# One row of weights ahead in the mixing, kept low parts and regrouped loads, in a two-layer hybrid decoder kernel

## The chip, the core and the metric

The kernel runs on one core of one Trainium2 chip. The metric is device time in microseconds (us) from the start to the end of one execution; several runs are timed, and one execution more is taken with the hardware profiler. TensorE (PE) multiplies matrices and loads its weights beside that (PEld), VectorE (DVE), ScalarE (ACT) and GpSimd (POOL) do the elementwise work, and SyncE (SP) issues the transfers (DMAs).

## The reference

Two layers of a decoder trunk on 1024 tokens of width 1024, in float32. Each layer has a token mixing and a channel mixing, each between a norm before and a norm after, whose scale, shift and gate come from a condition vector `c` (adaLN):

```python
mod = silu(c) @ ada_w[l] + ada_b[l]                # 6 x 1024: shift, scale, gate, for each half
h = rms_norm(x, g_pre_mix[l]) * (1 + scale_m) + shift_m
q, k, v, u = split(h @ w_in[l] + b_in[l])          # widths 512, 128, 128, 512
attn = sliding_window_attention(rotary(q), rotary(k), v, sinks)   # window 128, 8 heads on 2
pool = causal_pool_mixer(u)                        # trailing means over 2/4/8/16 less the token
x = x + gate_m * rms_norm(concat(attn, pool) @ w_out[l], g_post_mix[l])
h = rms_norm(x, g_pre_ffn[l]) * (1 + scale_f) + shift_f
f = (silu(h @ w_gate[l]) * (h @ w_up[l])) @ w_down[l]             # inner width 2816
x = x + gate_f * rms_norm(f, g_post_ffn[l])
```

## The kernel before

Every product of float32 matrices is made of three matmuls on parts: `split` rounds a tile to its high part `hi` on ScalarE (L213) and subtracts it from the tile on VectorE, which leaves the low part `lo` (L214); `mm3` adds high x high, high x low and low x high in one accumulator (L239, L242, L243). `weight` loads one row block of weights (128 rows) into a part of a `raw` tile and splits it. `raw`, `hi` and `lo` tiles are handed out in parts by `part`: there are two `raw` tiles of four 512-wide parts, and three `hi` and three `lo` tiles of two parts. Accumulators are four banks `acc` of PSUM, and smaller products share three banks `msc`.

The 1024 tokens are worked on in two halves of 512. In each layer the stages follow one another as generators, which `run` interleaves step by step:

- `dense0`: query and key/value projections of half 0 (`q_pass`, `kv_pass`).
- `dense`: `u_pass` of half 0 (the pooling mixer's input), then `kv_pass` and `q_pass` of half 1, 20 blocks of weight rows in all, with the attention of half 0 and the pooling mixer (`pool_mix`) between their steps. L797 to L822 are the softmax, L928 to L938 the pooling's sums.
- `out0`: the output projection of half 0 (`natural_proj`, called by `mix_out`), in two column halves `nh` of eight steps `k`. Each step splits a block of `w_out` and the block `left[k]` of the concatenated attention and pooling results, again for the second column half. The attention of half 1 is interleaved.
- `u_pass` of half 1, with the attention of half 1 and the norm of half 0 behind it; then first products of the channel mixing (`firsts`), and `out1`, the output projection of half 1.
- The rest of `firsts`, beside the norm of half 1 and `up_sums`, which builds for eight blocks the sums and differences of token halves (in pairs, on VectorE at L997 and L1002, on GpSimd at L1000 and L1004) that the products by seven instead of eight use, and splits them.
- `ups`: 11 pairs of columns of the up and gate weights, five products each (`up_pair`): raw weights of a pair are loaded (L1071), summed on VectorE (L1101, L1102, L1106, L1107), split and multiplied.
- `down`: the down projection by seven products. Its operand B11 is loaded into tiles `hT` by six loads (L1147), which are written in the last pair of `ups`.

The adaLN vectors of later stages are a stream of their own at the side (`side`): `ada_sum` loads blocks of `ada_w` into two `ar` tiles of 256 KB each and adds them up on VectorE, scaled by a column of `c_act` (L271, L273).

Each engine takes its instructions from a queue in a fixed order. That order is not the order of the text: the program builder schedules the instructions when the kernel is built, by data dependencies, free tiles and its own costs. `after(ins, prev)` forces one instruction to stand behind another.

In `q_pass`, `kv_pass` and `u_pass`, a row block is loaded and split in the step that multiplies by it, except for the first two passes of layer 0, which ask one step ahead (`ahead`).

## Time and profile before

| | us |
|---|---|
| Runs, median (each) | 1931.88 (1932.43, 1927.65, 1931.88) |
| The profiled execution's own time | 1928.41 |
| Span of the profile | 1926.6 |
| TensorE busy | 1867.8 (97%) |
| VectorE busy | 1559.5 (81%) |
| ScalarE busy | 949.8 (49%) |
| GpSimd busy | 49.1 (3%) |

Busy is the time in which an engine has an instruction at work; shares are of the span. Matmuls overlap in the pipeline, so a step between the starts of two matmuls is shorter than one matmul's duration. In the trace's rows the bracket behind an instruction tells how long its engine was idle before it and what it waited for.

### The profile page before, as it was taken

The numbers are of one execution on the slowest core, as the hardware profiler recorded it, in microseconds if no ns is written. First come the engines' busy times: TensorE is split into PE (matmuls) and PEld (weight loads), VectorE is DVE, ScalarE is ACT, GpSimd is POOL, SyncE is SP. The second block draws the span as 40 slices with busy tenths as digits, with TensorE's granted clock in tenths as the row PEclk, the third lists the DMA queues.
The fourth block names the chain that finished last, engine by engine and source line by source line (L and its number), as shares of the span: only waits on it lengthen the run. The fifth ranks groups of instructions, "written<-read, shape, count | busy, mean of one in ns | idle before, by whom it ended". The sixth has DMA issues, their size and how long they took to land.

```text
span 1926.6 us, 26083 instructions
## 1 busy us (share of the span) xinstructions
PE 1867.8 (97%) x8978; PEld 1540.6 (80%) x8978; DVE 1559.5 (81%) x2906; ACT 949.8 (49%) x1789; POOL 49.1 (3%) x100
## 2 busy tenths in 40 slices
PE   6999999999999999999999999999999999999997
PEld 4787778887788888888887878788878888888886
DVE  5889976758889898788878998756788888867687
ACT  4775785654222223445658667755622222235452
POOL 1000000011000000000000000000200000000000
PEclk9999999999999999999999999999999999999999
DMA  9345563558445565844554465536684555474342
GB/s 327 98 154 152 156 227 119 180 168 282 161 164 195 177 212 182 295 147 147 170 168 136 123 179 176 174 110 202 199 276 153 187 196 180 150 252 156 115 151 101
DMA packets 227428, 341.86 MB, mean 177 GB/s; under 512 B 16952, under 2 KB 124360, under 8 KB 227296
## 3 DMA queue, kind: packets, MB, share of 16 engines
q1 hardware_dynamic: 227152, 340.17, 53.8%
q8 instruction: 70, 1.15, 0.2%
q14 instruction: 62, 0.51, 0.1%
q0 software_dynamic: 32, 0.00, 0.0%
q10 hardware_dynamic: 112, 0.04, 0.0%
HBM read 267.25 MB, written 72.89 MB: 177 GB/s over the span
## 4 chain that ended last, share of the span: by engine, by line
PE 74%; DVE 12%; DMA 6%; ACT 4%; issue 2%; POOL 0%; SPq 0%; DVEq 0%; ACTq 0%; POOLq 0%
PE acc L243 23%; PE acc L239 22%; PE acc L242 22%; DMA ar<-in_ada_w_dram 3%; DVE lo L214 2%; DVE ada L273 1%; DMA raw<-in_w_up_dram 1%; PE msc L832 1%; ACT hi L213 1%; PE msc L502 1%; PE pv L239 1%; PE pv L242 1%; DMA ar<-x 1%; DVE fn L541 1%; PE pv L243 1%
## 5 line engine op out<-in xcount | busy, mean ns | idle before, releaser
L213 ACT ACTIVATE hi<-raw 128x1024 fp32r<-128x1024 f32 (+1 forms) x388 | 332.2, 868 | 374.5 <-PE acc L242 203.1
L214 DVE TENSOR_TENSOR lo<-raw,hi 128x1024 fp32r<-128x1024 f32 (+1 forms) x388 | 381.2, 989 | 122.6 <-ACT hi L213 122.1
L243 PE MATMUL acc<-t,lo 128*128 128x512 f32 x704 | 275.4, 391 | 5.0 <-DVE lo L214 5.0
L239 PE MATMUL acc<-t,hi 128*128 128x512 f32 x704 | 275.0, 391 | 1.6 <-ACT hi L213 1.6
L242 PE MATMUL acc<-t,hi 128*128 128x512 f32 x704 | 274.6, 390 | 0.0
L239 PE MATMUL acc<-bh,hi 128*128 128x512 f32 x520 | 202.7, 390 | 0.0
L243 PE MATMUL acc<-bh,lo 128*128 128x512 f32 x520 | 202.4, 389 | 0.0
L239 PE MATMUL acc<-hT,hi 128*128 128x512 f32 x480 | 190.6, 397 | 8.7 <-ACT hi L213 6.5
L242 PE MATMUL acc<-hT,hi 128*128 128x512 f32 x480 | 188.0, 392 | 0.0
L243 PE MATMUL acc<-hT,lo 128*128 128x512 f32 x480 | 186.2, 393 | 0.8 <-DVE lo L214 0.7
L1086 DVE TENSOR_TENSOR fn<-acc,fn 128x512 f32<-128x512 f32 x220 | 150.3, 683 | 42.6 <-PE acc L243 42.1
L243 PEld LDWEIGHTS acc<-t,lo 128*128 128x128 f32 x704 | 132.5, 188 | 35.0 <-DVE lo L214 7.6
L239 PEld LDWEIGHTS acc<-t,hi 128*128 128x128 f32 x704 | 132.6, 188 | 30.7 <-ACT hi L213 3.1
L242 PEld LDWEIGHTS acc<-t,hi 128*128 128x128 f32 x704 | 132.5, 188 | 27.7
L242 PE MATMUL acc<-ph,hi 128*128 128x512 f32 x320 | 124.6, 389 | 0.0
L273 DVE SCALAR_TENSOR_TENSOR ada<-ar,c_act,ada 128x512 f32<-128x512 f32 x140 | 104.4, 746 | 18.0 <-DMA ar<-in_ada_w_dram 16.7
L1024 ACT ACTIVATE fn<-fn 128x512 f32<-128x512 f32 x44 | 27.8, 633 | 177.3 <-DVE fn L1086 177.3
L243 PEld LDWEIGHTS acc<-bh,lo 128*128 128x128 f32 x520 | 97.6, 188 | 20.4
L239 PEld LDWEIGHTS acc<-bh,hi 128*128 128x128 f32 x520 | 97.6, 188 | 20.2
L239 PEld LDWEIGHTS acc<-hT,hi 128*128 128x128 f32 x480 | 90.3, 188 | 28.8 <-ACT hi L213 8.8
L243 PEld LDWEIGHTS acc<-hT,lo 128*128 128x128 f32 x480 | 89.8, 188 | 20.4 <-DVE lo L214 2.5
L242 PEld LDWEIGHTS acc<-hT,hi 128*128 128x128 f32 x480 | 90.3, 188 | 16.8
(306 smaller groups left out, 3870.9 us busy)
## 6 DMA issues: line engine op xcount, KB each, us to landing
ar<-in_ada_w_dram SPq DMA_DIRECT2D x160, 256.0 KB
raw<-in_w_gate_dram SPq DMA_DIRECT2D x44, 512.0 KB
raw<-in_w_up_dram SPq DMA_DIRECT2D x44, 512.0 KB
raw<-in_w_in_dram SPq DMA_DIRECT2D x80, 256.0 KB
raw<-keeps SPq DMA_DIRECT2D x40, 512.0 KB
keeps<-fn SPq DMA_DIRECT2D x66, 256.0 KB
two_b<-in_w_down_dram SPq DMA_DIRECT2D x30, 512.0 KB
raw<-keepa SPq DMA_DIRECT2D x25, 512.0 KB
```

The lines of the kernel that those rows point to most:

```text
L213: nc.scalar.activation(hi, src, AF.Copy)
L214: nc.vector.tensor_sub(lo, src, hi.bitcast(F32))
L239: ins = nc.tensor.matmul(dst, lh, rh, start=first, stop=False)
L242: nc.tensor.matmul(dst, lh, rl, start=False, stop=False)
L243: return nc.tensor.matmul(dst, ll, rh, start=False, stop=last)
L273: nc.vector.scalar_tensor_tensor(acc, w, c_act[:, i : i + 1], acc, op0=ALU.mult, op1=ALU.add)
L502: ins = nc.tensor.transpose(bank[:, t * P : (t + 1) * P], src[t], ident)
L541: nc.vector.scalar_tensor_tensor(fn[t][:, cs], fn[t][:, cs], rstd[:, t : t + 1], xs[t][:, cs], op0=ALU.mult, op1=ALU.add)
L832: nc.tensor.transpose(bank[:, i * P : (i + 1) * P], s[:, ii, ck * P : (ck + 1) * P], ident)
L1024: nc.scalar.activation(g, g, AF.Silu)
L1086: nc.vector.tensor_add(halves_of(dst)[m], bank, halves_of(src)[m])
```

## The change

Five edits:

1. `split` remembers its VectorE instruction, and every accumulation of `ada_sum` is forced behind the split that was written last.
2. `one_ahead` takes a list of row blocks across the borders of passes and hands out one at each step, after having loaded and split the next. All passes of the mixing take their rows from it.
3. `natural_proj` keeps the low parts of `left[k]`, `k` under 6, of the first column half in tiles `uT` and `pt`, and makes only their high parts again in the second.
4. The two GpSimd subtractions of `up_sums` go to VectorE.
5. The six loads of B11 are written one in each of the last six pairs of `ups`, each forced behind that pair's last raw load.

```diff
+    recent = {}
+
     def split(hi, lo, src):
 
         nc.scalar.activation(hi, src, AF.Copy)
-        nc.vector.tensor_sub(lo, src, hi.bitcast(F32))
+        recent["split"] = nc.vector.tensor_sub(lo, src, hi.bitcast(F32))
...
+    def one_ahead(makers):
+
+        makers = iter(makers)
+        held = [next(makers)()]
+
+        def ask():
+            now_ = held.pop()
+            for make in makers:
+                held.append(make())
+                break
+            return now_
+
+        return ask
...
-                    nc.vector.tensor_scalar(acc, w, c_act[:, 0:1], None, op0=ALU.mult)
+                    ins = nc.vector.tensor_scalar(acc, w, c_act[:, 0:1], None, op0=ALU.mult)
                 else:
-                    nc.vector.scalar_tensor_tensor(
+                    ins = nc.vector.scalar_tensor_tensor(
                         acc, w, c_act[:, i : i + 1], acc, op0=ALU.mult, op1=ALU.add
                     )
+                after(ins, recent["split"])
...
         K = len(left)
+        lows = {}
         for nh in range(2):
...
                 wh, wl = weight(*wsrc(k, nh))
-                lh, ll = part("hi"), part("lo")
-                split(lh, ll, left[k])
+                lh = part("hi")
+                if k in lows:
+                    ll = lows[k]
+                    nc.scalar.activation(lh, left[k], AF.Copy)
+                else:
+                    if nh == 0 and k < 6:
+                        lows[k] = t_("uT" if k < 4 else "pt", [P, HALO + T], F32R)[:, :T]
+                    ll = lows[k] if k in lows else part("lo")
+                    split(lh, ll, left[k])
...
-    def u_pass(l, h, hT, cols, uts, piece_read):
+    def u_pass(l, h, hT, cols, uts, piece_read, ask):
         banks = [acc_bank() for _ in range(4)]
         for k in range(KD):
-            wh, wl = weight((ALLP, None, w_in[l, k * P : (k + 1) * P, QKV:INW]))
+            wh, wl = ask()
...
-        nc.gpsimd.tensor_sub(f0, f1, f0)
+        nc.vector.tensor_sub(f0, f1, f0)
         split(*ops[T3][k], f0)
         nc.vector.tensor_sub(f1, f1, b11)
         split(*ops[T2][k], f1)
-        nc.gpsimd.tensor_sub(b21, b21, f1)
+        nc.vector.tensor_sub(b21, b21, f1)
...
+        ask = one_ahead(
+            (all_rows(q_rows, l) + all_rows(kv_rows, l, 2) if l else [])
+            + all_rows(u_rows, l) + all_rows(kv_rows, l, 2) + all_rows(q_rows, l)
+        )
...
-        run(u_pass(l, 1, pieces, cols, uts[1], lambda k, ins: None), KD, (att, 10), (pre, KD))
+        ask1 = one_ahead(all_rows(u_rows, l))
+        run(u_pass(l, 1, pieces, cols, uts[1], lambda k, ins: None, ask1), KD, (att, 10), (pre, KD))
...
-                    if p == NPAIR - 1 and i == 1:
-                        for g in range(len(DOWN_GROUPS)):
-                            load(B11, g)
+                    g = p - (NPAIR - len(DOWN_GROUPS))
+                    if g >= 0 and i == 1:
+                        after(load(B11, g), recent["raw"])
                     yield
```

Line numbers of the changed kernel are higher: L216 there is L214 of before, L287 and L289 are L271 and L273, L816 to L841 are L797 to L822, L947 to L957 are L928 to L938, L696 is L667, L1023 is L1004, L1044 is L1025, L1073 is L1054, L1122, L1123, L1127 and L1128 are L1101, L1102, L1106 and L1107.

The order of instructions on VectorE, first in `dense` of layer 0, where `u_pass` ends and the row blocks of `kv_pass` are wanted. Before:

```order
L932 SCALAR_TENSOR_TENSOR pt<-pt,uT 128x512
L797 ISA sb,st<-msc,mask 128x256
L797 ISA st 128x1
L737 TENSOR_TENSOR vz<-qkv,vz 128x64 x2
L797 ISA sb,st<-msc,mask 128x256
L797 ISA st 128x1
L817 TENSOR_TENSOR st<-st 128x4
L937 TENSOR_TENSOR pt<-pt,rcnt 128x16
L273 SCALAR_TENSOR_TENSOR ada<-ar,c_act,ada 128x512
L818 RECIPROCAL st<-st 128x4
L938 TENSOR_TENSOR pt<-pt,uT 128x16
L214 TENSOR_TENSOR lo<-raw,hi 128x512
```

In the changed kernel, the rows that lead up to the same softmax (`vz`, L756 there, is L737):

```order
L216 TENSOR_TENSOR lo<-raw,hi 128x512
L828 SCALAR_TENSOR_TENSOR st<-st,sk 128x4
L947 TENSOR_TENSOR pt<-pt 128x525
L831 TENSOR_TENSOR st<-st,sk 128x4
L947 TENSOR_TENSOR pt<-pt 128x521
L756 TENSOR_TENSOR vz<-qkv,vz 128x64 x2
L816 ISA sb,st<-msc,mask 128x256
L816 ISA st 128x1
L816 ISA sb,st<-msc,mask 128x256
L816 ISA st 128x1
L951 SCALAR_TENSOR_TENSOR pt<-pt,uT 128x512
L216 TENSOR_TENSOR lo<-raw,hi 128x512
```

The low part of a row stands ahead of the pooling's last sums and of the softmax's reciprocal, and no accumulation of adaLN stands between the two low parts.

Second, on VectorE at the end of the first `kv_pass` of layer 1, where the bias is added to keys and values (L667). Before:

```order
L484 TENSOR_SCALAR cfb<-sa,rs 128x1024
L484 TENSOR_SCALAR cfb<-sb,rs 128x1024
L273 SCALAR_TENSOR_TENSOR ada<-ar,c_act,ada 128x512 x2
L214 TENSOR_TENSOR lo<-raw,hi 128x512
L273 SCALAR_TENSOR_TENSOR ada<-ar,c_act,ada 128x512 x2
L667 TENSOR_TENSOR qkv<-acc,bqkv 128x256 x4
```

And in the changed kernel (L501 is L484):

```order
L501 TENSOR_SCALAR cfb<-sa,rs 128x1024
L501 TENSOR_SCALAR cfb<-sb,rs 128x1024
L289 SCALAR_TENSOR_TENSOR ada<-ar,c_act,ada 128x512
L696 TENSOR_TENSOR qkv<-acc,bqkv 128x256 x4
L739 TENSOR_TENSOR rt<-qkv,cos_t 128x80
```

Three accumulations and the split of a row no longer stand ahead of the bias additions; that split stands further up.

Third, on VectorE at the start of `ups`, where the first sums of the up weights are made. Before:

```order
L1025 TENSOR_TENSOR sb<-sb 128x512
L1101 TENSOR_TENSOR raw<-raw 128x8x128
L271 TENSOR_SCALAR ada<-ar,c_act 128x512
L1102 TENSOR_TENSOR raw<-raw 128x8x128
L273 SCALAR_TENSOR_TENSOR ada<-ar,c_act,ada 128x512
L1106 TENSOR_TENSOR raw<-raw 128x8x128
L214 TENSOR_TENSOR lo<-raw,hi 128x1024
L273 SCALAR_TENSOR_TENSOR ada<-ar,c_act,ada 128x512
```

And in the changed kernel:

```order
L1044 TENSOR_TENSOR sb<-sb 128x512
L1122 TENSOR_TENSOR raw<-raw 128x8x128
L1123 TENSOR_TENSOR raw<-raw 128x8x128
L1127 TENSOR_TENSOR raw<-raw 128x8x128
L216 TENSOR_TENSOR lo<-raw,hi 128x1024
L1073 TENSOR_TENSOR sb<-acc,sa 128x512
L1128 TENSOR_TENSOR raw<-raw 128x8x128
L1073 TENSOR_TENSOR sb<-acc,sa 128x512
```

The accumulations between the sums and the low part are gone from this place; the first of them stands some rows further down.

## Rows read from the trace of the kernel before

**Rows 1.** The engines' busy time over the span, with instruction counts (first part of the profile's page).

```profile
PE 1867.8 (97%) x8978; PEld 1540.6 (80%) x8978; DVE 1559.5 (81%) x2906; ACT 949.8 (49%) x1789; POOL 49.1 (3%) x100
```

**Rows 2.** Stretches of the span: from and to, length, busy us (instructions) of TensorE, its weight loads, VectorE, ScalarE and GpSimd, then the granted clock of TensorE (1.00 is full), the busy share of the DMA engines and what they moved in GB/s. The first two, the sixth and the seventh lie in the mixing of the two layers; the third is the time before the up products of layer 0, the fourth their start, the fifth their long part, and the last their start in layer 1.

```profile
62.00:170.00 108.00, 101.16 (x634) 86.45 (x634) 98.08 (x295) 78.80 (x195) 4.92 (x13) 0.98 0.42 125
...
201.00:236.00 35.00, 33.73 (x184) 26.98 (x183) 33.50 (x88) 26.06 (x68) 0.42 (x2) 1.00 0.53 166
...
415.00:455.00 40.00, 40.00 (x190) 33.34 (x190) 36.52 (x46) 25.54 (x41) 11.39 (x8) 1.00 0.69 210
455.00:500.00 45.00, 42.08 (x176) 33.37 (x175) 38.51 (x51) 13.83 (x16) 0.00 (x0) 0.96 0.73 250
500.00:950.00 450.00, 450.00 (x2001) 372.23 (x2000) 382.09 (x516) 165.05 (x237) 0.00 (x0) 1.00 0.56 189
1014.00:1048.00 34.00, 31.70 (x191) 26.20 (x191) 32.10 (x106) 28.77 (x70) 0.00 (x0) 1.00 0.35 99
...
1148.00:1181.00 33.00, 31.83 (x170) 26.26 (x171) 28.97 (x81) 24.22 (x63) 0.48 (x2) 1.00 0.44 137
...
1400.00:1445.00 45.00, 41.36 (x177) 33.02 (x178) 39.00 (x50) 13.62 (x16) 0.00 (x0) 1.00 0.81 279
```

**Rows 3.** TensorE's waits by line and what they waited for: us in total, times, the longest.

```profile
PE acc L239 <- ACT hi L213: 9.9, 10, 2.2
PE acc L243 <- DVE lo L214: 5.6, 7, 1.1
PE msc L832 <- DVE sb L822: 5.2, 7, 1.3
```

**Rows 4.** TensorE's timeline at the places that the prediction speaks of: start, duration, instruction, in brackets the idle time before it and its releaser.

```profile
83.99 0.50 PE L239 MATMUL acc<-hT,hi 128*128 128x512 f32 x1 [2.18 <-ACT hi L213]
...
84.57 0.39 PE L239 MATMUL acc<-hT,hi 128*128 128x512 f32 x1
84.79 0.40 PE L242 MATMUL acc<-hT,hi 128*128 128x512 f32 x1
...
150.39 0.50 PE L242 MATMUL acc<-lo,hT 128*128 128x512 f32 x1 [2.32 <-DVE lo L214]
...
151.31 0.67 PE L239 MATMUL msc<-hi,pwh 128*128 128x512 f32 x1
...
154.33 0.63 PE L242 MATMUL acc<-lo,hT 128*128 128x512 f32 x1
...
456.16 0.50 PE L239 MATMUL acc<-t,hi 128*128 128x512 f32 x1 [0.76 <-ACT hi L213]
...
458.95 0.63 PE L243 MATMUL acc<-t,lo 128*128 128x512 f32 x1
...
461.51 0.63 PE L243 MATMUL acc<-t,lo 128*128 128x512 f32 x1
...
1015.38 0.50 PE L239 MATMUL acc<-hT,hi 128*128 128x512 f32 x1 [1.47 <-DVE qkv L667]
...
1149.17 0.50 PE L239 MATMUL acc<-hi 128*128 128x512 f32 x1 [1.47 <-ACT hi L213]
```

**Rows 5.** VectorE's timeline in `dense` of layer 0, up to the low part that the matmul of 150.39 waits for, in the same columns.

```profile
143.09 0.75 DVE L273 SCALAR_TENSOR_TENSOR ada<-ar,c_act,ada 128x512 f32<-128x512 f32 x1 [1.35 <-DMA ar<-in_ada_w_dram]
...
146.42 0.74 DVE L273 SCALAR_TENSOR_TENSOR ada<-ar,c_act,ada 128x512 f32<-128x512 f32 x1
...
148.84 0.74 DVE L273 SCALAR_TENSOR_TENSOR ada<-ar,c_act,ada 128x512 f32<-128x512 f32 x1
...
149.65 0.68 DVE L214 TENSOR_TENSOR lo<-raw,hi 128x512 fp32r<-128x512 f32 x1
150.25 0.87 DVE L822 TENSOR_SCALAR sb<-sb,st 128x256 f32<-128x256 f32 x3
```

**Rows 6.** ScalarE's timeline ahead of the high part that the matmul of 83.99 waits for.

```profile
79.43 1.28 ACT L813 ACT_TABLE_LOAD   x1
...
83.33 0.61 ACT L213 ACTIVATE hi<-raw 128x512 fp32r<-128x512 f32 x1
```

**Rows 7.** VectorE's timeline in layer 1 ahead of the matmul of 1015.38.

```profile
1012.76 0.75 DVE L273 SCALAR_TENSOR_TENSOR ada<-ar,c_act,ada 128x512 f32<-128x512 f32 x1 [1.32 <-DMA ar<-in_ada_w_dram]
...
1014.58 1.41 DVE L667 TENSOR_TENSOR qkv<-acc,bqkv 128x256 f32<-128x256 f32 x4
```

**Rows 8.** VectorE's low parts of `left[k]` by their operands, over the whole span: count, durations in ns (least, median, greatest), first and last start.

```profile
L214 DVE TENSOR_TENSOR lo<-cfa,hi x32: 661/681/687, 167.3 to 1172.2; 128x512 fp32r<-128x512 f32 x32
L214 DVE TENSOR_TENSOR lo<-cfb,hi x32: 679/684/694, 316.2 to 1301.8; 128x512 fp32r<-128x512 f32 x32
```

**Rows 9.** The timeline of all engines in `up_sums` of layer 0, where GpSimd and VectorE work at the same time.

```profile
428.24 1.67 POOL L1004 TENSOR_TENSOR ar<-ar,sa 128x512 f32<-128x512 f32 x1 [0.80 <-DVE sa L1002]
428.68 2.38 DVE L214 TENSOR_TENSOR t<-sa,t 128x512 fp32r<-128x512 f32 x2
...
430.99 0.68 DVE L214 TENSOR_TENSOR t<-ar,t 128x512 fp32r<-128x512 f32 x1
```

**Rows 10.** VectorE's timeline at the start of `ups` in layer 0.

```profile
452.26 1.23 DVE L1101 TENSOR_TENSOR raw<-raw 128x1024 f32<-128x1024 f32 x1 [0.57 <-DMA raw<-in_w_up_dram]
...
454.94 0.75 DVE L273 SCALAR_TENSOR_TENSOR ada<-ar,c_act,ada 128x512 f32<-128x512 f32 x1
```

More of the change, by code (lines that the diff above doesn't have):

```diff
@@ L633, in hybrid_decoder_kernel, with kv_rows, q_rows, u_rows @@
     attn = {}
-    def kv_pass(l, hT, par, qkvs, pairs=None):
+    def kv_rows(l, k):
+        return weight(
+            (ALLP, 2, w_in[l, k * P : (k + 2) * P, ATT:QKV].rearrange("(a p) n -> p a n", p=P))
+        )
+    def q_rows(l, k):
+        return weight((ALLP, None, w_in[l, k * P : (k + 1) * P, 0:ATT]))
+    def u_rows(l, k):
+        return weight((ALLP, None, w_in[l, k * P : (k + 1) * P, QKV:INW]))
+    def all_rows(rows, l, step=1):
+        return [lambda k=k: rows(l, k) for k in range(0, KD, step)]
+    def kv_pass(l, hT, par, qkvs, ask, pairs=None):
         banks = pairs or [acc_bank() for _ in range(2)]
         dsts = [banks[t // 2][:, t % 2 * 256 : t % 2 * 256 + 256] for t in range(NT)]
-        def rows(k):
-            return weight(
-                (ALLP, 2, w_in[l, k * P : (k + 2) * P, ATT:QKV].rearrange("(a p) n -> p a n", p=P))
-            )
-        ahead = None
-        if pairs:
-            ahead = rows(0)
-            yield
         for k in range(KD):
             if k % 2 == 0:
-                (wh, wl), ahead = ahead or rows(k), None
-            elif pairs and k + 1 < KD:
-                ahead = rows(k + 1)
+                wh, wl = ask()
             cs = slice(k % 2 * 256, k % 2 * 256 + 256)
@@ L667, in kv_pass, with q_pass @@
             nc.vector.tensor_add(qkvs[t][:, ATT:QKV], dsts[t], par["bq"][:, ATT:QKV])
-    def q_pass(l, hT, par, qkvs, first=False):
+    def q_pass(l, hT, par, qkvs, ask):
         banks = [acc_bank() for _ in range(NT)]
-        def rows(k):
-            return weight((ALLP, None, w_in[l, k * P : (k + 1) * P, 0:ATT]))
-        ahead = None
-        if first:
-            ahead = rows(0)
-            yield
         for k in range(KD):
-            wh, wl = ahead or rows(k)
-            ahead = rows(k + 1) if first and k + 1 < KD else None
+            wh, wl = ask()
             hi, lo = hT[k]
@@ L688, in q_pass @@
             nc.vector.tensor_add(qkvs[t][:, 0:ATT], banks[t], par["bq"][:, 0:ATT])
-    def u_pass(l, h, hT, cols, uts, piece_read):
+    def u_pass(l, h, hT, cols, uts, piece_read, ask):
         banks = [acc_bank() for _ in range(4)]
         for k in range(KD):
-            wh, wl = weight((ALLP, None, w_in[l, k * P : (k + 1) * P, QKV:INW]))
+            wh, wl = ask()
             for g in range(4):
@@ L1070, in up_pair @@
             for m, w in enumerate((w_gate, w_up)):
-                nc.sync.dma_start(raws[kh][:, m * HK : (m + 1) * HK, :], up_rows(w, l, kh, 2 * p, 2 * p + 2))
+                recent["raw"] = nc.sync.dma_start(
+                    raws[kh][:, m * HK : (m + 1) * HK, :], up_rows(w, l, kh, 2 * p, 2 * p + 2)
+                )
         (a11, a21), (a12, a22) = ((r[:, :, 0:P], r[:, :, P : 2 * P]) for r in raws)
@@ L1146, in load @@
             w = t_(tag, [P, p1 - p0, 512])
-            nc.sync.dma_start(w, rows[odd][:, p0:p1, dh * 512 : (dh + 1) * 512])
             wd[name].append(w)
+            return nc.sync.dma_start(w, rows[odd][:, p0:p1, dh * 512 : (dh + 1) * 512])
         return wd, load
@@ L1363, in dense0 @@
         def dense0():
-            yield from q_pass(l, hts[0], par, qkvs[0]) if l else queries0
-            yield from kv_pass(l, hts[0], par, qkvs[0]) if l else keys0
+            yield from q_pass(l, hts[0], par, qkvs[0], ask) if l else queries0
+            yield from kv_pass(l, hts[0], par, qkvs[0], ask) if l else keys0
+        ask = one_ahead(
+            (all_rows(q_rows, l) + all_rows(kv_rows, l, 2) if l else [])
+            + all_rows(u_rows, l) + all_rows(kv_rows, l, 2) + all_rows(q_rows, l)
+        )
         side = ada_jobs(l)
@@ L1373, in dense @@
         def dense():
-            yield from u_pass(l, 0, hts[0], cols, uts[0], piece_read)
-            yield from kv_pass(l, pieces, par, qkvs[1])
-            yield from q_pass(l, pieces, par, qkvs[1])
+            yield from u_pass(l, 0, hts[0], cols, uts[0], piece_read, ask)
+            yield from kv_pass(l, pieces, par, qkvs[1], ask)
+            yield from q_pass(l, pieces, par, qkvs[1], ask)
         def pool0():
```

7 lines of the change are left out of this document (3 added, 4 removed).

## The prediction

> **What bounds the kernel now.** I read the engines' busy time first: TensorE is busy for 1867.8 of 1926.6 us [rows 1], so nothing can gain more than its idle or slow stretches, some 59 us, of which the start and the end of the program take a part that the change doesn't touch. The second view is the table of stretches [rows 2]. In the up products' long part (500 to 950 us) TensorE shows 450.00 busy us of 450, and nothing done there for VectorE or the queues can be seen in the time. It idles in the mixing (62 to 236 in layer 0, 1014 to 1181 in layer 1: 6.84, 1.27, 2.30 and 1.17 us in the four stretches shown) and for the first 45 us of the up products (2.92 in layer 0, 3.64 in layer 1). In the same stretches VectorE is 98.08 of 108 us busy, 33.50 of 35 and 32.10 of 34: nearly full, but not the engine that is always ahead of TensorE in the chain. The third view, TensorE's waits, says by whom it is held: the high parts of a split (ScalarE, L213) 9.9 us in 10 waits, their low parts (VectorE, L214) 5.6 us in 7, and beside these the scaled probabilities of the softmax (L822) 5.2 us in 7 [rows 3]. The fourth, TensorE's timeline, gives each of these waits a place [rows 4].
>
> What the reader is to see in it: the waits come where a pass begins, or where a row of weights is split only as it is wanted, behind other work in the queue of ScalarE or VectorE. The matmul of 150.39 waited 2.32 us for a low part. On VectorE that subtraction started at 149.65, right behind adaLN accumulations of 143.09, 146.42 and 148.84, the first of which had waited 1.35 us for its DMA [rows 5]. The matmul of 83.99 waited 2.18 us for a high part that ScalarE began at 83.33, behind a table load of 1.28 us and a softmax [rows 6]. A wait costs twice: after that of 150.39 the granted clock fell to its lower level, 1.2 of 2.4 GHz, for a while. The matmuls from 151.31 to 154.33 start 0.43 us apart, where those behind 84.57 start 0.22 apart, and the stretch's mean clock is 0.98 [rows 2, 4].
>
> **The change, part by part.** *Rows one step ahead, and adaLN operations behind the last split.* The order of VectorE in layer 0 shows the low part of the next row ahead of the softmax's closing operations, and no accumulation between it and the low part before. The two waits of this place are 2.18 + 2.32 = 4.5 us, and the slow matmuls 7 steps x (0.43 - 0.22) = 1.5 us more: 6.0 us. I take 5.0, since ScalarE's table load and softmax still stand there and may take a part; bounds 0 and 6.0. In layer 1 the matmul of 1015.38 waits 1.47 us for the bias additions L667, which start at 1014.58 behind accumulations, of which the first waited 1.32 us for its DMA [rows 4, 7]. In the new order one accumulation is left ahead of them instead of two and a split and two. I take 1.0, bounds 0 and 1.47.
>
> *Low parts kept.* It takes 6 subtractions from each of four output projections, 24 of 0.68 us each [rows 8], 16 us of VectorE's work. The kept tiles are the pooling mixer's, idle by then. Only where TensorE idles can that be worth something: the projection of half 0, with 1.27 us idle in layer 0 and 1.17 in layer 1 [rows 2]; in that of half 1 TensorE has nothing to gain, and the saving there is hidden by TensorE's own matmuls. The high part still has to be made again, on ScalarE, and the wait of 1149.17, at the change of column halves in layer 1, is one for such a high part [rows 4], which a kept low part doesn't shorten by itself; so I take half, 1.2 us for both layers, bounds 0 and 2.4.
>
> *The start of the up products.* Three parts meet here. The accumulations go behind the splits: in the order of before two of them stand between the sums L1101, L1102, L1106 and the low part that follows, one of them 0.75 us long [rows 10]; in the new order none. The loads of Down's B11, which the order of before issues all six beside the first raw loads, where the DMA engines are busy for 0.73 and 0.81 of the stretch against 0.56 in the long part [rows 2], are spread over six pairs, each behind that pair's raw weights. The last of them is issued before Down's other operands, so nothing of Down waits that did not before; I cost it at nothing, covered by an up stage in which TensorE is full. And the GpSimd subtractions stop holding back VectorE (next paragraph). What is there to win: 2.92 + 3.64 us idle [rows 2] and in layer 0 the slow matmuls from 458.95 to 461.51, 6 steps x 0.21 = 1.2 us [rows 4], 7.8 us in all. The first wait of 456.16 (0.76 us) stays, since the sum ahead of it waits 0.57 us for the raw weights of the up projection [rows 10], and something similar in layer 1. I take 5.0, bounds 0 and 7.8.
>
> *Subtractions from GpSimd to VectorE.* 8 more per layer, just ahead of that start. One of this size takes VectorE 0.68 us and starts the next after 0.60 [rows 5, 9]: 8 x 0.60 = 4.8 us, where VectorE is 36.52 of 40 us busy [rows 2], so 3.48 are free, and 1.3 would not fit. Against it stand VectorE's own operations that lengthen while GpSimd works: the pair of subtractions at 428.68 takes 2.38 us, beside a GpSimd operation of 1.67 that began at 428.24, where one alone takes 0.68 [rows 9]: 2 x 0.60 + 0.08 = 1.28 would be normal, so 1.1 us are lost by that one. With half of the eight losing as much, 4.4 us come back, about the cost. TensorE is 40.00 of 40 us busy there, and that is the cover: more coming back would show in no time. I take 0 for both layers; bounds 0 and a loss of 2 x 1.3 = 2.6, which is counted in the second rival below.
>
> Here a rule speaks against the change. The Trainium skill (Perfetto Trace Analysis, section Optimizing Scalar/DVE Operations) would move work the other way, off a saturated VectorE even to GpSimd, though it adds that the two share a port and this might not help. By its first half the part would cost the upper bound, and the sum below would be 2.6 us higher, 1920.3. Another page of the Trainium skill (SBUF — State Buffer, section Who interferes with whom) lets a VectorE operation with two SBUF inputs and a GpSimd operation that reads SBUF shut each other out; by it the sum stays as it is, and the 2.38 us agree.
>
> *What it adds.* The split of a row ahead stands in VectorE's queue in front of a softmax's operations, for which TensorE already waits 5.2 us in 7 waits [rows 3]. If each of the seven comes 0.60 later, that is 4.2 us; the accumulations that went back make room for some, and I take 1.5. Bounds 0 and 6, the upper end for as many places again where such a chain just fits now. Each row held ahead also takes a place of the three `hi` and three `lo` tiles for longer; the kept low parts free some.
>
> **The sum.** 5.0 + 1.0 + 1.2 + 5.0 - 1.5 = 10.7 us less than the profiled execution's 1928.4 gives 1917.7. That execution lies 3.5 us under the median of the runs, 1931.88 (1927.65 to 1932.43), from which the same gain leads to 1921.2. I predict 1919, some 0.7% faster. What a measurement of this kernel can tell from no change is 0.3%, 5.8 us: below 1926.1 counts as faster, above 1937.7 as slower.
>
> **Rivals.** *More than that.* VectorE's load is what holds the mixing, and relieving it of 16 us of subtractions and of its waits for DMA lets all idle time close: 11.6 us in the four mixing stretches, 1.5 of slow matmuls, 7.8 at the up start, 20.9 in all, so 1907.5. For it speaks that VectorE is over 90% busy in these stretches; against it, that the relief stands in the projections and not in the dense passes, where TensorE idles most.
>
> *The waits only change places.* With VectorE 91% busy from 62 to 170, what is pulled ahead pushes something back: the softmax is late by the upper bound of 6, and the subtractions do not fit (2.6), so of the 12.2 us gained 3.6 are left: 1924.8 by the profiled execution, 1928.3 by the median. For it speaks that three kinds of waits with three releasers are spread over the same places [rows 3]; against it, that the low part pulled ahead is one operation of 0.68 us, and that three of what stood before it in [rows 5] are accumulations of adaLN, whose sum is wanted only when all eight of its terms are in.
>
> *Slower.* The ring of `hi` and `lo` decides. Three tiles of two 512-wide parts serve the rows of the dense passes, and also the attention's and the pooling's splits between them. A row held ahead leaves these one part less; a split that finds none waits until TensorE has finished a row, and then has a high part and a low part to make, some 1.2 us (0.61 and 0.68, the latter's next operation starting after 0.60 [rows 5, 6]). The two dense streams have 20 rows each. From 10 such waits on (12 us) the gain is gone; at 18, 21.6 us against 12.2 give 9.4 more than now, 1938 to 1941. Against it: what TensorE waits for now are splits that were begun late, behind other work [rows 5, 6], not for want of a part, and the changed projections ask for fewer.
>
> **How the numbers follow.** Forecast 0.62 (1911 to 1926: all bounds of the gains at their best give 1928.4 - 17.7, and half of the sum, taken from the median, gives the upper end), more 0.10, changing places 0.19, slower 0.09. The first two lie below 1926.1: faster 0.72, same 0.19, slower 0.09. The range goes from 1906, just under the rival with more, to 1933, where the waits that change places are taken in with the run to run spread; it leaves out the slower case and half of the larger gain, 0.14.
>
> **What would show it.** Right: in the trace of after no wait over 1 us of a dense row for L214's or L213's counterpart around 84 and 150 us, and no matmuls 0.43 us apart behind them; an idle time of some 2 us instead of 2.92 and 3.64 at the up start; VectorE's two-operation group near 428 at 1.28. Wrong: TensorE's waits for the softmax's scaled probabilities at over 9 us in place of 5.2; waits of ScalarE for a free `hi` part; new idle time in the long up part behind the spread loads; the stretch before the up start no longer 40.00 of 40 us full on TensorE.

## The result, and the profile after

The changed kernel takes 1913.61 us (median of four runs, 1913.29 to 1917.83), the kernel before 1929.77 in its runs beside it (1926.16 to 1932.43): a ratio of 0.9919, 95% interval 0.9903 to 0.9936. The forecast was 1919, between 1906 and 1933, and faster. The direction came out, and the size within the range; how the sum came about did not, and most of this part is on that.

The profiled execution has a span of 1912.0 us. Busy times per engine (compare [rows 1]):

```profile
PE 1866.7 (98%) x8978; PEld 1540.9 (81%) x8978; DVE 1544.5 (81%) x2898; ACT 949.6 (50%) x1789; POOL 24.0 (1%) x84
```

TensorE did the same work in 14.6 us less. To see where, both spans are cut at equal amounts of TensorE's work: matmuls are counted with the step that they have in the full pipeline (0.23 us for 512 columns, 0.12 for 256, 0.06 for 128), and a stretch lies between two sums of these. In layer 0 the first three stretches below are the dense passes, the first part of what follows them (the projection of half 0 and the start of the u pass of half 1), and the start of the up products; the next three are the same of layer 1, the dense passes there with the end of the stage before. Columns as in [rows 2]; first the kernel before, then the changed one.

```profile
65.34:163.92 98.58, 91.74 (x579) 78.44 (x578) 89.08 (x274) 74.67 (x186) 4.25 (x11) 0.98 0.40 121
163.92:231.30 67.38, 64.78 (x337) 51.89 (x335) 64.07 (x168) 44.34 (x108) 1.09 (x4) 1.00 0.57 174
444.97:510.84 65.87, 62.95 (x268) 50.65 (x266) 55.99 (x72) 19.12 (x24) 1.86 (x2) 0.97 0.71 242
975.48:1112.14 136.66, 131.60 (x804) 113.33 (x803) 122.34 (x341) 91.88 (x228) 6.77 (x19) 1.00 0.49 148
1112.14:1180.70 68.56, 65.06 (x340) 52.67 (x339) 61.71 (x165) 45.73 (x112) 0.88 (x4) 1.00 0.54 165
1394.12:1459.32 65.20, 61.51 (x267) 49.35 (x266) 56.27 (x71) 17.90 (x23) 0.00 (x0) 1.00 0.71 241
```

```profile
65.83:155.18 89.35, 89.02 (x574) 77.02 (x572) 85.78 (x264) 73.91 (x185) 2.19 (x11) 1.00 0.41 122
155.18:226.90 71.72, 67.59 (x342) 53.59 (x341) 64.81 (x173) 45.46 (x110) 1.28 (x5) 0.98 0.63 188
439.30:499.54 60.24, 60.24 (x268) 49.82 (x267) 49.01 (x64) 16.90 (x21) 0.00 (x0) 1.00 0.58 189
965.91:1097.12 131.21, 130.04 (x799) 112.78 (x797) 118.49 (x333) 90.88 (x225) 5.69 (x17) 1.00 0.49 151
1097.12:1170.50 73.38, 68.33 (x346) 53.87 (x345) 62.60 (x166) 46.62 (x114) 1.70 (x5) 0.98 0.53 163
1383.04:1443.11 60.07, 60.07 (x267) 49.76 (x265) 49.27 (x61) 15.85 (x18) 0.00 (x0) 1.00 0.51 168
```

The dense passes are 9.2 and 5.5 us shorter, the starts of the up products 5.6 and 5.1, and at these starts TensorE is busy for the whole stretch. What follows each is longer: 4.3 and 4.8 us in the two stretches behind the dense passes (2.7 and 3.5 when the stretch is drawn to the end of the first products, as in the table below). Of these 4.3 and 4.8 us only 1.5 and 1.6 are idle time of TensorE; 2.8 and 3.3 are longer busy time, with the granted clock at 0.98 where it was 1.00.

Of TensorE's waits over the span, those for a low part (`lo`) fell most, from 8.3 us (5.6 in [rows 3] and 2.7 in the first line here) to 0.2; those for a high part fell from 9.9 to 5.4, those for the softmax from 5.2 to 3.4. Those for the next attention's keys (L774 is L755 of before) grew from 2.2 us, with 0.3 for a high part, to 3.9, and those for the projection's evictions (L638 is L612) from 0.6 to 2.3. Lines of the kernel before, then of the changed one:

```profile
PE acc L242 <- DVE lo L214: 2.7, 2, 2.3
PE msc L755 <- DVE rt L723: 1.9, 2, 1.3
PE acc L239 <- DVE fn L612: 0.6, 2, 0.3
```

```profile
PE acc L255 <- ACT hi L215: 5.4, 9, 1.1
PE msc L851 <- DVE sb L841: 3.4, 5, 1.3
PE acc L255 <- DVE fn L638: 2.3, 4, 1.0
PE msc L774 <- DVE rt L742: 2.0, 1, 2.0
PE msc L774 <- DVE hi L769: 1.9, 1, 1.9
PE acc L259 <- DVE lo L216: 0.2, 1, 0.2
```

The two waits of over 2 us of [rows 4] are gone, and the slow matmuls with them (a granted clock of 1.00 in the dense passes of layer 0, where it was 0.98). In the dense passes of layer 0 one wait of 0.3 us is left.

### The profile page after: what moved, and what is told of

Read it like the earlier page. It is cut to its first block, busy times and chain, and to the rows that moved or that the text cites. A ratio compares the mean times of both kernels' runs of the same rounds, so it can differ in the third digit from the quotient of the medians.

```text
span 1912.0 us, 26078 instructions
## 1 busy us (share of the span) xinstructions
PE 1866.7 (98%) x8978; PEld 1540.9 (81%) x8978; DVE 1544.5 (81%) x2898; ACT 949.6 (50%) x1789; POOL 24.0 (1%) x84
## 4 chain that ended last, share of the span: by engine, by line
PE 77%; DVE 12%; DMA 6%; ACT 3%; issue 2%; SPq 0%; DVEq 0%; ACTq 0%
PE acc L255 23%; PE acc L259 23%; PE acc L258 23%; DVE lo L216 2%; DMA ar<-in_ada_w_dram 2%; DMA raw<-in_w_up_dram 2%; DVE ada L289 1%; PE msc L851 1%; ACT hi L215 1%; PE msc L519 1%; DVE fn L1107 1%; PE pv L255 1%; DMA ar<-x 1%; PE pv L258 1%; PE msc L813 1%
## 5 line engine op out<-in xcount | busy, mean ns | idle before, releaser
L216 DVE TENSOR_TENSOR lo<-raw,hi 128x1024 fp32r<-128x1024 f32 (+1 forms) x388 | 379.9, 986 | 122.8 <-ACT hi L215 119.8
L1107 DVE TENSOR_TENSOR fn<-acc,fn 128x512 f32<-128x512 f32 x220 | 150.2, 684 | 37.2 <-PE acc L259 37.2
L289 DVE SCALAR_TENSOR_TENSOR ada<-ar,c_act,ada 128x512 f32<-128x512 f32 x140 | 104.6, 747 | 11.1 <-DMA ar<-in_ada_w_dram 10.1
L255 PEld LDWEIGHTS acc<-hT,hi 128*128 128x128 f32 x480 | 90.2, 188 | 21.3 <-ACT hi L215 3.5
L255 PE MATMUL acc<-hi 128*128 128x512 f32 x256 | 102.4, 406 | 2.8 <-DVE fn L638 1.7
```

The lines of the kernel that those rows point to most:

```text
L216: recent["split"] = nc.vector.tensor_sub(lo, src, hi.bitcast(F32))
L255: ins = nc.tensor.matmul(dst, lh, rh, start=first, stop=False)
L289: ins = nc.vector.scalar_tensor_tensor(acc, w, c_act[:, i : i + 1], acc, op0=ALU.mult, op1=ALU.add)
L1107: nc.vector.tensor_add(halves_of(dst)[m], bank, halves_of(src)[m])
```

## The experiments

All runs were also cut at equal work. The table gives, against the first trace of the kernel before, by how many us each stretch is shorter (-) or longer, and "all" is the sum over all stretches (without the program's start and end, so it differs from the difference of the spans by up to 1.0). "Behind" is the stretch from the end of the dense passes to the end of the first products; "later" runs from behind the up start to near the end of the down products. The stretch that is left out in each layer, with the projection of half 1 in it, differs by at most 0.7 in any run. The medians come from several groups of runs; the kernel before, timed beside each, had medians from 1927.65 to 1930.52, so a difference of under some 3 us between two of these medians tells little.

| run | dense 0 | behind 0 | up start 0 | later 0 | dense 1 | behind 1 | up start 1 | later 1 | all | median us |
|---|---|---|---|---|---|---|---|---|---|---|
| changed kernel | -9.2 | 2.7 | -5.6 | 1.7 | -5.5 | 3.5 | -5.1 | 2.1 | -14.6 | 1913.6 |
| e_noahead | -3.7 | 3.5 | -5.6 | 3.0 | -0.7 | 3.8 | -5.1 | 1.7 | -2.1 | 1927.6 |
| e_noada | -5.7 | 1.9 | -5.5 | 2.1 | -4.2 | 1.6 | -4.0 | 0.0 | -12.8 | 1915.6 |
| e_pool | -8.9 | 3.5 | -3.9 | 2.9 | -5.6 | 5.1 | -1.0 | 3.2 | -3.7 | 1923.6 |
| e_b11 | -8.4 | 3.3 | -5.6 | 1.2 | -5.5 | 4.8 | -4.3 | 2.8 | -10.9 | 1917.1 |
| e_nolow | -9.3 | 3.4 | -5.6 | 0.9 | -6.0 | 4.6 | -5.1 | 3.0 | -14.0 | 1914.5 |
| n_adamix | -8.9 | 3.2 | -5.5 | 2.3 | -5.5 | 5.0 | -2.0 | 0.0 | -10.3 | 1917.5 |
| n_late | -8.5 | 12.8 | -5.1 | -0.1 | -6.0 | 5.0 | -3.4 | 0.1 | -4.4 | 1923.7 |
| n_rot | -7.7 | 3.9 | -5.6 | 2.7 | -5.5 | 3.2 | -5.1 | 3.5 | -9.8 | 1916.5 |
| s_ahead | -6.6 | 2.8 | -0.9 | 2.0 | -5.2 | 1.7 | 0.7 | 0.1 | -5.3 | 1922.7 |
| s_dve | -2.5 | 0.1 | -1.3 | -0.1 | -1.2 | -0.9 | -2.3 | 0.1 | -8.1 | 1920.6 |
| s_pair | -7.7 | 1.0 | -3.3 | 1.1 | -5.2 | 2.3 | -2.4 | 0.0 | -14.1 | 1916.1 |
| b_again | 0.1 | 0.7 | -0.1 | 0.2 | -0.5 | -0.4 | 0.1 | -0.0 | 0.2 | 1929.1 |

**The accumulations' forced order taken out** (e_noada).

```diff
-                after(ins, recent["split"])
```

> The changed kernel, with the accumulations of adaLN no longer forced behind the last split; all else stays. TensorE's idle time over its work, summed by place, says that the change took 10.8 us away at the two starts of the up products (5.6 in layer 0, 5.2 in layer 1), and that 3.9 us of new waits appear later in the up products, in front of high parts. Theory A: the forced order does both, since no accumulation stands between the sums and the low part any more and they pile up later. Then the starts get back 8 to 11 us, the later waits (3.9) go, and the kernel takes 1918 to 1921. Theory B: the loads of B11 that no longer crowd the first raw loads did it. Then this run takes 1911 to 1915, and the starts stay at under 1 us of idle time. Theory C: the subtractions moved from GpSimd did it: as B here.

1915.57 us (1913.43 to 1916.85), ratio to before 0.9922 (0.9902 to 0.9942), which can't be told from the changed kernel. Theory A falls: the starts of the up products stay short. The time lies between A and B. The forced order is worth 3.5 and 1.3 us in the dense passes and 1.1 at the start of layer 1, and costs part of that behind the dense passes (0.8 and 1.9) and, in layer 1, later (2.1).

**Rows split when wanted** (e_noahead). In `ask`, `held` stays empty for `dense` and `ask1`, and `now_` is `next(makers)()`.

> The changed kernel, with each row of weights of dense and of the u pass of half 1, and in layer 1 of the first two passes too, loaded and split in the step that multiplies by it, as in the kernel before; the forced order of the accumulations stays. In layer 0 the dense passes lost 9.2 us of idle time and 3.8 came back at once at the keys of the next attention; in layer 1 it is 5.4 and 5.0. Theory A (the row split ahead brings it): the waits of 2.2 to 2.3 us for a high and a low part come back near 83 and 148 us, the ones for the keys go, and the kernel takes 1918 to 1922. Theory B (accumulations out of the way of the splits bring it, the row ahead adds little): no wait over 1 us there, and 1912 to 1916.

1927.61 us, ratio 0.9995 (0.9982 to 1.0007): next to nothing is left of the gain (2.1 us by the table). The wait of 2.18 us is back at its old place, and one like it in layer 1 (TensorE's timeline):

```profile
83.42 0.49 PE L255 MATMUL acc<-hT,hi 128*128 128x512 f32 x1 [2.18 <-ACT hi L215]
...
1026.86 0.51 PE L255 MATMUL acc<-hT,hi 128*128 128x512 f32 x1 [2.17 <-ACT hi L215]
```

Theory A was too small for the time, and holds for one of its two places: the wait of 2.32 us near 150 us did not come back (the longest there is 0.49), and the wait in layer 1 is one that the kernel before did not have. Its waits for keys should have gone with the rows ahead; they stayed (3.5 and 3.8 us behind the dense passes), so it isn't the rows ahead alone that are paid back there.

**The subtractions back on GpSimd** (e_pool).

```diff
-        nc.vector.tensor_sub(f0, f1, f0)
+        nc.gpsimd.tensor_sub(f0, f1, f0)
...
-        nc.vector.tensor_sub(b21, b21, f1)
+        nc.gpsimd.tensor_sub(b21, b21, f1)
```

> The changed kernel, with the two subtractions of the sums of halves back on GpSimd. Theory A (forced order): TensorE stays full before the up products and their start stays below 1 us of idle time: 1912 to 1916. Theory C (these subtractions were what made the start late): idle time of 2 us or more comes back at each start, 1917 to 1922. VectorE's operations beside GpSimd's should take up to 1.1 us longer for two than the 1.28 that they take now, under either.

1923.59 us, ratio 0.9959 (0.9945 to 0.9974): 10 us more than the changed kernel, the largest part but the rows, and theory C, though TensorE's idle time at the starts is 1.3 and 1.9 us and not 2. By the table 5.8 us of the loss lie at the two starts and 2.3 later; 2.6 lie in the mixing, where every engine has the order of the changed kernel, and stay open.

Two chains meet at the first sum. One is VectorE's own: beside GpSimd a pair of its subtractions takes 2.38 us again, once it waits 1.17 us for GpSimd, and it ends the operation ahead of the sum at 446.06:

```profile
421.84 0.69 DVE L1021 TENSOR_TENSOR sa<-sa,ar 128x512 f32<-128x512 f32 x1 [1.17 <-POOL sa L1019]
...
423.05 2.38 DVE L216 TENSOR_TENSOR t<-sa,t 128x512 fp32r<-128x512 f32 x2
...
435.04 0.68 DVE L216 TENSOR_TENSOR t<-ar,t 128x512 fp32r<-128x512 f32 x1
...
445.37 0.69 DVE L1044 TENSOR_TENSOR sb<-sb 128x512 f32<-128x512 f32 x1
446.89 1.23 DVE L1122 TENSOR_TENSOR raw<-raw 128x1024 f32<-128x1024 f32 x1 [0.82 <-DMA ar<-in_ada_w_dram]
```

The other is SyncE's: the last load into an `ar` tile goes out only when VectorE has made the low part of 435.04, which reads this tile behind GpSimd's subtraction in it, and the raw weights of the first pair stand behind that load, and here behind three other transfers too:

```profile
435.75 0.34 SPq L1015 DMA_DIRECT2D ar<-h  x1
...
437.78 0.41 SPq L1090 DMA_DIRECT2D raw<-in_w_gate_dram  x1
```

In the changed kernel, whose stretch begins at the same time (439.30, here 439.37), that load is issued 1.0 us and the weights 2.1 us earlier, VectorE is ready for the sum at 443.13, and the sum starts 3.4 us earlier:

```profile
434.71 0.39 SPq L1015 DMA_DIRECT2D ar<-h  x1
435.67 0.38 SPq L1090 DMA_DIRECT2D raw<-in_w_gate_dram  x1
```

```profile
442.45 0.68 DVE L1044 TENSOR_TENSOR sb<-sb 128x512 f32<-128x512 f32 x1
443.48 1.23 DVE L1122 TENSOR_TENSOR raw<-raw 128x1024 f32<-128x1024 f32 x1 [0.35 <-issue]
```

The sum reads `raw` only, so the transfer that it waits for is taken to be that of the weights, though the bracket names another. Then of the 3.4 us only the 0.82 of waiting is held by the transfer alone; VectorE would have been some 2.5 us late with the weights there. In layer 1 the sum waits 1.39 us for the weights:

```profile
1391.05 1.23 DVE L1122 TENSOR_TENSOR raw<-raw 128x1024 f32<-128x1024 f32 x1 [1.39 <-DMA raw<-in_w_up_dram]
```

No run takes one chain out without the other.

**B11's loads together again** (e_b11): the two lines of `ups` as they were before.

> The changed kernel, with the six loads of B11 written together in the last pair again, without a forced place, so that the builder puts them among the first raw loads of the up products. Theory A: the DMA engines are busier at the start, but nothing waits: 1912 to 1916. Theory B: TensorE waits for sums that wait for raw loads, 2 to 5 us at each start, 1917 to 1923.

1917.09 us (1916.58 to 1919.73), ratio 0.9935 (0.9918 to 0.9952). The time fits theory B, the place doesn't: the start keeps its 5.6 us in layer 0 and 4.3 of 5.1 in layer 1. A part of what is missing (1.3 us behind the dense passes of layer 1) stands where every engine has the order of the changed kernel. Spreading the loads brings at most some 3.5 us, and through which wait stays open.

**Low parts not kept** (e_nolow).

```diff
-                    if nh == 0 and k < 6:
+                    if False:
```

> The changed kernel without kept low parts: the 24 subtractions (0.60 us of VectorE's queue each) are back. Theory A (VectorE's queue holds the projections of half 0): the two waits for evictions at the change of column halves in layer 1 (1.0 and 1.2 us) and the other waits of these stages grow by 1 to 2.5 us over both layers, 1914.5 to 1917. Theory B (the projections have room for them, kept parts free the tiles and let TensorE run into the evictions sooner): those two waits go, a wait for a high part of 1.5 us takes their place, and the time stays at 1912 to 1915.

1914.49 us, ratio 0.993 (0.9903 to 0.9956): the time of theory B, without its reason, since the two waits for evictions in layer 1 stay (1.3 us, 1.7 in the changed kernel). The 14 us of subtractions saved on VectorE bring 0.6 us by the table and nothing that can be measured.

**Only the rows ahead on the kernel before** (s_ahead): the changed kernel with the other four edits taken out as above.

> The kernel before with only the rows of weights one step ahead; accumulations, low parts, GpSimd subtractions and loads of B11 as before. Without the forced order, the changed kernel stood 3.0 us lower in the mixing of layer 0 and 2.5 lower in that of layer 1 than before; without the rows ahead, 0.4 us lower and 0. Theory A (the rows ahead bring it, and the forced order adds the rest on top of them): 5 to 6 us faster than before in the mixing, starts of the up products as before: 1921 to 1925. Theory B (one does nothing without the other): 1926 to 1930.

1922.73 us, ratio 0.9966 (0.9952 to 0.998). Theory A: the dense passes shorten by 6.6 and 5.2 without any help. The waits for the softmax in those of layer 0 are not what the rows take away. First the kernel before, then this run, then the changed kernel without the forced order, and last, in two lines, without the rows ahead:

```profile
PE msc L832 <- DVE sb L822: 1.6, 3, 1.0
```

```profile
PE msc L851 <- DVE sb L841: 1.6, 2, 1.4
```

```profile
PE msc L851 <- DVE sb L841: 2.4, 3, 1.4
```

```profile
PE msc L851 <- DVE sb L841: 0.5, 1, 0.5
...
PE msc L851 <- DVE st L816: 0.2, 1, 0.2
```

The runs with the accumulations forced behind the splits have 0.3 (the changed kernel) and 0.7, those without it 0.8 (s_pair) to 2.4.

**Only the subtractions on VectorE on the kernel before** (s_dve).

> The kernel before with only the two subtractions of up_sums moved from GpSimd to VectorE. The changed kernel with them put back on GpSimd had 1.8 us more idle time on TensorE at the start of the up products in layer 0, 4.1 in layer 1 and 2.2 in the later waits. Theory A (the chain to the first sums is shorter by itself): 4 to 7 us faster than before, 1922 to 1925, with the mixing unchanged. Theory B (the chain is short only if the accumulations and loads are out of its way too): 1926 to 1930, with the waits of 1.1 us for a low part still at the start of the up products.

1920.57 us, ratio 0.9957 (0.9941 to 0.9972): faster than theory A. But only 3.6 of the 8.1 us lie at the starts. 2.5 lie in the dense passes of layer 0, where all engines have the order of before: there the accumulation of [rows 5] waited for its block of weights 0.24 us instead of 1.35, and the matmul of 150.39 for 1.27 instead of 2.32 (VectorE, then TensorE):

```profile
142.33 0.75 DVE L273 SCALAR_TENSOR_TENSOR ada<-ar,c_act,ada 128x512 f32<-128x512 f32 x1 [0.24 <-DMA ar<-in_ada_w_dram]
```

```profile
149.68 0.50 PE L242 MATMUL acc<-lo,hT 128*128 128x512 f32 x1 [1.27 <-DVE lo L214]
```

**These two together, nothing else** (s_pair).

> The rows one step ahead and the subtractions on VectorE, nothing else of the change. Theory A (these two carry it, the sum of both alone): the run with the rows alone, 1922.7, less what the subtractions bring, 1915 to 1919; the forced order, the kept low parts and the spread loads are left 2 to 5 us together. Theory B (the start of the up products needs all): 1920 to 1924.

1916.09 us, ratio 0.993 (0.9913 to 0.9947), theory A: these two edits carry the change, and the other three bring at most 2 to 3 us on top. By the table these three gain 6.8 us in the dense passes and at the starts and give 5.6 back behind and later.

**The kernel before once more** (b_again).

> The kernel before, unchanged, for a second trace of it. The run with only the subtractions moved has the same order of instructions on every engine in the mixing as the kernel before, and yet its trace shows 2.4 us less idle and slow time there in layer 0 and 2.1 less in layer 1. Theory A (that is the spread between two executions, from the arrival of transfers and the clock that falls or doesn't): this trace differs from the first one of before by 1 to 3 us in the mixing, above all at the wait of 2.3 us near 150 us and the slow matmuls behind it, and by under 0.5 us at the starts of the up products; the time is within 0.2% of the other runs of before. Theory B (the moved subtractions change the mixing too, by what they leave in the queues): under 0.7 us of difference in the mixing.

1929.07 us, ratio 1.0003 (0.9993 to 1.0012). No stretch differs by more than 0.7 us from the first trace; the accumulation of [rows 5] waits for its block as before, here 1.41 us:

```profile
143.69 0.75 DVE L273 SCALAR_TENSOR_TENSOR ada<-ar,c_act,ada 128x512 f32<-128x512 f32 x1 [1.41 <-DMA ar<-in_ada_w_dram]
```

So these two executions of one kernel differ little, by theory B's number, and the 2.5 us of the run with only the subtractions moved look like more than ordinary spread, as far as two traces tell. But theory B's reason isn't shown either: nothing in that stretch was moved. Why the block landed sooner there stays open.

**Forced order in the mixing only** (n_adamix).

```diff
-                after(ins, recent["split"])
+                after(ins, recent["split"]) if recent.get("mix") else None
```

> The changed kernel with the forced order of the accumulations in the mixing only, not in the up products. The waits for high parts that came up there (0.9 and 0.5 us in layer 0, 0.7 and 0.9 in layer 1, 4 us in all with the matmuls slow behind them) were gone in the run without the forced order, where other waits of 1.2 and 0.9 us for a low part stood instead. Theory A (the pile of accumulations that were pushed back makes those waits): 2 to 4 us less than the changed kernel, 1909.5 to 1911.5. Theory B (they only change places): 1912 to 1915.

1917.53 us, ratio 0.994 (0.9919 to 0.9962): slower than either theory gave. The waits for high parts go, and two for low parts stand in the start of layer 1, which loses 3.1 us of its gain. So the waits change places, and these places are worse, though the later stretch of layer 1 gets its 2.1 us back. The two new waits:

```profile
1420.96 0.50 PE L259 MATMUL acc<-t,lo 128*128 128x512 f32 x1 [1.23 <-DVE lo L216]
...
1428.04 0.50 PE L259 MATMUL acc<-t,lo 128*128 128x512 f32 x1 [1.03 <-DVE lo L216]
```

**The attention of half 1 one step later** (n_late, on top of the run above).

```diff
-        run(out0, 2 * KD, (side, 4 * ADA), (att, 16))
+        next(out0); run(out0, 2 * KD - 1, (side, 4 * ADA), (att, 15))
```

> As the run with the forced order in the mixing only, and the attention of half 1 begins one step of the projection of half 0 later. In the changed kernel TensorE waits 2.1 us in each layer for its keys, which stand in TensorE's queue behind the first step of the projection, while their rotary parts on VectorE wait for the bias additions of the queries. Theory A (these waits are what the row ahead gave back): they go, and the run takes 3 to 4 us less than the one with the forced order in the mixing only, 1906 to 1908. Theory B (VectorE's queue is full there, and the wait moves to the next softmax): no difference beyond 1.5 us from that run.

1923.71 us, ratio 0.9971 (0.9956 to 0.9985): both theories fall. The edit also starts the adaLN stream of this stage a step later, so it is not the attention alone that moved. In layer 0 the wait for the keys is still 1.4 us, and new ones of up to 2.2 us for a split of adaLN (L387) and a softmax (L851) come up (waits from 155 to 307 us); the stretch behind the dense passes is 9.6 us longer than without the shift:

```profile
PE msc L387 <- ACT ph L215: 3.2, 2, 2.2
PE msc L851 <- DVE sb L841: 2.7, 2, 2.2
PE msc L774 <- DVE hi L769: 1.4, 1, 1.4
```

**The first rotary part earlier** (n_rot, on the changed kernel).

```diff
             nc.vector.tensor_add(qkvs[t][:, 0:ATT], banks[t], par["bq"][:, 0:ATT])
+            if t == 0 and first is not None:
+                att_rotary(first, qkvs[0])
```

> The changed kernel, with the rotary part of the first block of half 1 written right behind the first bias addition of its queries, so that on VectorE it stands ahead of the three other additions and of the accumulations between them. In the changed kernel TensorE waits 2.1 us in each layer for this block's keys. Theory A (the rows ahead gave back there what VectorE's queue order costs): both waits go or fall under 0.7 us, 1910 to 1912. Theory B (the keys also wait for a high part on ScalarE and for other work in front, or the next wait takes its place): 1912.5 to 1915.

1916.46 us (1912.16 to 1918.76), ratio 0.9926 (0.9909 to 0.9942). Theory B in kind, and slower than it gave: in layer 0 the wait for keys (first line, the changed kernel) goes, and others stand in its stead, for a split of adaLN and for an accumulation (second fence, this run):

```profile
169.21 0.53 PE L774 MATMUL msc<-ident,hi 128*128 128x128 f32 x4 [1.95 <-DVE hi L769]
```

```profile
167.36 0.40 PE L387 MATMUL msc<-ph,picks 128*4 128x512 f32 x1 [1.50 <-ACT ph L215]
...
199.18 0.54 PE L800 MATMUL msc<-ident,hi 128*128 128x128 f32 x4 [1.38 <-DVE ada L289]
```

In that stretch of the changed kernel VectorE is busy for 64.81 of 71.72 us and TensorE for 67.59. Whether what stands behind the dense passes is VectorE's load or the order in its queue, these runs don't tell apart: three changes of the order (n_late, n_rot, and the forced order taken out) gave 10.1, 1.2 and -0.8 us against the changed kernel there in layer 0.

## Why the prediction came out

The direction and the likeliest case were right, and the net, 10.7 us forecast, is 14.6 by the spans and 16 by the medians. Term by term:

- **Dense passes.** 5.0 and 1.0 us were forecast, with upper bounds of 6.0 and 1.47; they gave 9.2 and 5.5. The step that failed is the bound. In layer 0 it added 4.5 us of waits for a split and 1.5 of slow matmuls; TensorE's idle time fell by 6.5 and its busy time by 2.7. In layer 1 it took one wait of 1.47; idle time fell by 3.9 and busy time by 1.6. A part of this are the waits for the softmax in layer 0 (1.6 to 0.3 us), which the forecast had counted as a cost; the rows alone do not take these away (1.6 stay), and the runs with the forced order have the fewest (0.3 and 0.7). The mechanism itself is shown for the wait of 2.18 us: it is back when the rows are split as they are wanted, and gone with the rows alone. The wait of 2.32 us goes with either of the two edits. Without the rows next to nothing of the net gain is left.
- **Start of the up products.** 5.0 forecast, bound 7.8; 10.7 came, of which 3.8 were given back later. Three causes were named there, and with the loads and the subtractions costed at nothing the weight lay on the accumulations between the sums. The run without the forced order refutes that: 9.5 of the 10.7 us stay. The subtractions, which I had costed at nothing, or a loss of 2.6, are worth 5.8 us at the two starts of the changed kernel, and 3.6 alone. The step that failed is the cover, that "more coming back would show in no time" where TensorE is 40.00 of 40 us busy. It is busy there, but what VectorE and SyncE are behind in that stretch is paid at its end: with the subtractions on GpSimd VectorE comes to the first sum 2.9 us and the raw weights go out 2.1 us later. The row of a GpSimd operation beside a lengthened VectorE one [rows 9] was read for VectorE's time in that stretch, not for what stands behind it. The first half of the Trainium skill's rule (Perfetto Trace Analysis, section Optimizing Scalar/DVE Operations), that it may make sense to take work off a saturated VectorE, would have had this part cost time; here VectorE at 36.52 of 40 us took the work and the kernel gained. The Trainium skill's other page (SBUF — State Buffer, section Who interferes with whom) led to no cost, which was nearer, but not to the gain.
- **Low parts.** 1.2 forecast, 0.6 by the table, inside the noise, so neither the size nor the half that was taken is borne out.
- **What it adds.** 1.5 forecast, bound 6. 2.7 + 3.5 us came back behind the dense passes and 1.7 + 2.1 later, 10 in all. The step that failed is the path: the term counted softmax operations that come later, and the waits for the softmax fell from 5.2 to 3.4 us. What came back are waits for keys, evictions and, later, high parts, and matmuls at a lower granted clock behind them. That is the rival in which waits change places, and it happened alongside the gains. The accumulations pushed back behind splits are a part of it: without the forced order 2.7 and 3.5 are 1.9 and 1.6, and the 2.1 later in layer 1 are 0.0 (in layer 0 the 1.7 are 2.1). The new waits in the long up part were named as a sign of being wrong; they do not come from the spread loads, for with the loads together 1.2 and 2.8 us stand there.
- **Spread loads.** Costed at nothing; up to 3.5 us, cause open.

So both sides of the sum were too small, gains of 12.2 that were 25.4 and a cost of 1.5 that was some 11. That the net came out near the forecast is luck: two errors of opposite sign. The slower rival, a want of `hi` and `lo` parts, did not decide: the dense passes, where it would have stood, are 14.7 us shorter together.

## What to carry to other kernels

A slow operation off the critical path is priced by what stands behind it, in the queues of the engine that it slows and of the one that waits for its tile: here GpSimd's subtractions made the first sum of the up products of layer 0 3.4 us late, by way of VectorE and of SyncE, though TensorE was full while they ran. Work that is brought forward in a full queue paid back 29 to 64% of its gain at the next place where the same engine feeds the critical one; forecast both sides. Where parts overlap, take each one out of the whole and put each one in alone: taken out they cost 14.0, 10.0, 3.5, 2.0 and 0.9 us by the medians (the last two inside the noise), nearly twice the 16 that all of them bring.

## What was not expected of the hardware

After the wait of 2.32 us the granted clock averaged 0.89 over the next 15 us of the kernel before; after 1.27 us at the same place (the run with only the subtractions moved) it stayed at 1.00, and with 1.05 us less of waiting the dense passes were 2.5 us shorter. The prediction said that a wait costs twice, and for its other wait that is not so: after the 2.18 us before the matmul of 83.99 the clock stayed at 1.00. In the changed kernel it fell behind a shorter one, the 1.95 us before the matmul of 169.21. So the length of the wait alone does not tell. The stretches of the kernel before at its two waits, of the run with only the subtractions moved, and of the changed kernel, each from close to the wait's end:

```profile
84.00:99.00 15.00, 14.82 (x99) 12.61 (x100) 13.00 (x43) 12.49 (x29) 0.00 (x0) 1.00 0.15 44
...
150.00:165.00 15.00, 13.74 (x66) 10.91 (x67) 13.26 (x34) 8.96 (x23) 0.00 (x0) 0.89 0.33 89
```

```profile
149.00:164.00 15.00, 13.45 (x74) 10.86 (x74) 14.76 (x37) 10.48 (x25) 0.00 (x0) 1.00 0.35 102
```

```profile
169.00:184.00 15.00, 14.73 (x68) 12.01 (x69) 13.78 (x35) 9.46 (x19) 0.00 (x0) 0.89 0.68 199
```
